# Re-tiling the keys of a causal attention by 128 from the first meta token, in a one-core decoder-block kernel

## The chip, the core and the metric

The kernel runs on one core of one Trainium2 chip. The core has a matrix engine (TensorE, PE in the profile; its weight loads are a row of their own, PEld), a vector engine (VectorE, DVE), a scalar engine (ScalarE, ACT), a general engine (GpSimd, POOL) and a queue engine that issues the transfers (SyncE, SP). The metric is the device time of one execution in microseconds (us). Before the change it is 1646.86 us, the median of 3 runs that lie between 1645.23 and 1648.12 us.

## What is computed

One decoder layer on 1024 tokens of width 1024 with 16 learned meta tokens put ahead of them, so 1040 positions: a norm, one wide projection, three mixers side by side (sliding-window attention with sinks, SWA; forgetting attention, FoX; a gated recurrence), gated sums of their outputs, and a SwiGLU feed-forward. The meta rows are dropped at the end. The change touches FoX, whose core in the reference is

```python
s = jnp.einsum('bqhd,bkhd->bhqk', qi, k).astype(jnp.float32) * (dh ** -0.5)
s = s + ci[..., :, None] - cum[:, :, None, :]
q_pos = n * BLOCK + jnp.arange(BLOCK)
mask = (k_pos[None, :] <= q_pos[:, None]) & (k_pos >= n_pad)[None, :]
s = jnp.where(mask, s, NEG_INF)
p = jax.nn.softmax(s, axis=-1).astype(v.dtype)
return jnp.einsum('bhqk,bkhd->bqhd', p, v)
```

It has 8 heads of 64 channels. Only the 1024 real tokens are queries of the kernel. Query block j holds the real tokens 128j to 128j+127, which are the positions 16+128j to 16+128j+127. With causality it needs the positions 0 to 143+128j: whole tiles of 128 counted from position 0, and 16 keys more, and these last 16 are seen by the last 16 queries of the block alone.

## The kernel before

All products of matrices are made from float32 data that is split in two parts, a rounded high part and the rest (`split`, lines 112 to 125: ACT copies the high part, DVE subtracts it). A projection is three products per tile, high by high, high by low, low by high (`mm3`, line 144, its matmul on line 151).

The part around the change runs from about 223 us to 734 us of the profiled execution. Two Python generators are woven into one program by `drive` (line 233). The main generator gives the projections: queries and keys of each pair of heads, and 24 gate tiles whose results go to memory. The side generator gives the attention, first SWA (mixer 0), then FoX (mixer 1). After each piece of the side (a `yield`), `drive` lets the main generator emit products until their estimated cost, in ns, has filled a gap: 850 in SWA, 480 in FoX (`GAPS`, line 40). A scheduler then sets the final order on each engine; the rows of order below are what it gives.

In FoX a head is worked in four blocks t of 256 queries (two query blocks i of 128 each). `fox_scores` (line 627) multiplies queries by keys, takes the running minimum of the negated scores on DVE, the exponential on ACT and the division by the sum on POOL (line 663); the result `s` has queries on partitions. `fox_values` (line 665) lists the key tiles, and `pv_pieces` (line 552) works them in groups: a group has a PSUM bank `tr`; each 128x128 tile of `s` is transposed into it (line 573); the bank is split into `ph` and `pl` (lines 118, 119 by way of line 576); and two groups later (`LAG`) each key tile is multiplied as `v` tile by `ph` and by `pl` into the bank `ob` (line 562). `v` has the high part of the values in 64 columns and the low part in the other 64, so a weight load of it has 128 columns. Key tile 0 is the 16 meta tokens alone, padded by zero rows of `v` (line 531 writes them on POOL), and key tile c is the positions 16+128(c-1) onwards, so that tile 2t+2 is the diagonal tile of the second query block, and one tile per block is mostly padding. The transposed scores of tile 0 are those of positions 0 to 127, of which rows 16 to 127 meet the zero rows.

A block t before has the tile 0 and the tile 2t+2 in a first group (3 transposes), then the tiles 1 to 2t+1 in groups of two (4 transposes each), the last of them alone (2 transposes): 4t+5 transposes, 2t+2 pairs of products with 256 columns and one pair with 128. Values come back from memory by `load_v` (line 525), two transfers per head on SP.

Of the kernel before, what the change touches and what calls it, by code (L numbers as in the profile page):

```python
# [9 lines left out]
F32 = mybir.dt.float32  # L10
# [6 lines left out]
P = 128  # L17
D = 1024
KT = D // P
NM = 16  # L20
# [16 lines left out]
P_CW, P_CB, P_BR, P_BI, P_LM, P_NF = 0, 16, 20, 24, 28, 32  # L37

LRU_GAP = 3500.0
GAPS = (850.0, 480.0)  # L40
CREDIT = 8
LAG = 2

# [3 lines left out]
def f32(ap):  # L47
    return ap.bitcast(F32)
# [3 lines left out]
def hybrid_block(ctx, tc, h_in, w_in, w_v0, w_v1, w_bd, par, rows, gains, relt, onehot,  # L52
# [51 lines left out]


    gz = dp.tile([24, P, S], F32, name="gz")
    vs = dp.tile([9, P, 10, P], F32, name="vs")
    osp = dp.tile([3, 2, 4, P, S], F32, name="osp")
    h1s = dp.tile([8, P, D], F32, name="h1s")
    cums = dp.tile([8, T], F32, name="cums")  # L110
# [339 lines left out]
    def values(i, src, ncol):  # L450
        vh = rv.tile([P, KT, ncol], F32R, tag="vh", bufs=1, name=nm("vh"))
        vl = rv.tile([P, KT, ncol], F32R, tag="vl", bufs=1, name=nm("vl"))
        for k in range(0, KT, 2):
            raw = wp.tile([P, 2 * ncol], F32, tag="wr", name=nm("wr"))
            dma(raw, src[:, k * ncol:(k + 2) * ncol])
            split(vh[:, k:k + 2], vl[:, k:k + 2], raw.rearrange("p (k c) -> p k c", k=2))
        for t in range(9):
            n = NM if t == 0 else P
            t0 = 0 if t == 0 else NM + (t - 1) * P
            c, off = (0, t0) if t0 < W0 else (1, t0 - W0)  # L460
            ps = mm_bank(f"_v{t}")
            if t == 0:

                for k in range(KT):
                    for a, b in ((meta[:, k], vh), (meta[:, k, :NM], vl)):
                        pe.matmul(ps[:a.shape[-1], :ncol], a, b[:, k], start=k == 0 and b is vh, stop=k == KT - 1,
                                  skip_group_check=True)
                    yield 2 * (ncol / 2.4 + 3)
                low = rv.tile([NM, ncol], F32, tag="low", bufs=1, name=nm("low"))
                act.activation(low, ps[32:32 + NM, :ncol], AF.Copy)  # L470
                dve.tensor_tensor(low, ps[:NM, :ncol], low, ALU.add)
                ps = low
            else:
                yield from mm3(ps[:, :ncol], [(uh[c][:, k, off:off + P], ul[c][:, k, off:off + P],
                                               vh[:, k], vl[:, k]) for k in range(KT)])
            st = rv.tile([P, 5, 2, 64], F32R, tag="vst", bufs=2, name=nm("vst"))
            split(st[:n, :, 0], st[:n, :, 1], ps[:n, :320].rearrange("p (h d) -> p h d", h=5))
            dma(vs[t, :n, 5 * i:5 * i + 5], st[:n].rearrange("p h a d -> p h (a d)"))
            if ncol > 320:
                dve.tensor_tensor(zall[:n, t], ps[:n, 320:328], rowt[:n, 8:16], ALU.add)  # L480

# [8 lines left out]
    with ExitStack() as ctx2:  # L490
# [33 lines left out]
                    dma(x[b], x[a])  # L524

        def load_v(h):

            v = at([P, 9, P], F32R, "v", 2)
            if h == 0:
                pad(r2, 320 + 5632)  # L530
            pool.memset(f32(v[:, 0]), 0.0)
            dma(v[:, 1:], vs[1:, :, h].rearrange("t p c -> p t c"))
            dma(v[:NM, 0], vs[0, :NM, h])
            return v

        def out_sum(ob, ot, h, q0, n):
# [14 lines left out]
        def pv_pieces(pieces, vt, ob):  # L551
# [5 lines left out]

            def pv(todo, ph, pl):
                nonlocal count
                for c, a, b, q0 in todo:  # L560
                    for x in (ph, pl):
                        pe.matmul(ob[:, q0:q0 + b - a], vt[:, c], x[:, a:b],  # L562
                                  start=count == 0, stop=count == n_mm - 1, skip_group_check=True)
                        count += 1

            for grp in pieces:
                tb = tr_bank()
                ph, pl = at([P, 512], F32R, "ph", 3), at([P, 512], F32R, "pl", 3)
                todo, col = [], 0
                for c, cols, q0 in grp:  # L570
                    w0 = col
                    for src in cols:
                        pe.transpose(tb[:, col:col + P], src, ident)  # L573
                        col += P
                    todo.append((c, w0, col, q0))
                split(ph[:, :col], pl[:, :col], tb[:, :col])
                pend.append((todo, ph, pl))
                yield None
                if len(pend) > LAG:
                    pv(*pend.pop(0))  # L580
                    yield None
# [82 lines left out]

        def fox_values(h, t, st, vt, ot):
            ob = o_bank()
            last = 2 * t + 2

            def piece(c):
                k0 = 0 if c == 0 else NM + P * (c - 1)  # L670
                if c == last:
                    return c, [st[1][:, k0:k0 + P]], P
                return c, [st[i][:, k0:k0 + P] for i in range(2)], 0

            pieces = [[piece(0), piece(last)]]
            pieces += [[piece(x) for x in range(c, min(c + 2, last))] for c in range(1, last, 2)]
            yield from pv_pieces(pieces, vt, ob)
            out_sum(ob, ot, h, 256 * t, 256)

# [618 lines left out]
```

## Time and profile before

| | before |
|---|---|
| median of 3 runs (lowest, highest) | 1646.86 us (1645.23, 1648.12) |
| the profiled execution's own time | 1646.19 us |
| its span, first to last instruction | 1644.4 us |
| PE busy | 1623.2 us, 99% |
| PEld busy | 1369.6 us, 83% |
| DVE busy | 997.7 us, 61% |
| ACT busy | 762.1 us, 46% |
| POOL busy | 387.4 us, 24% |
| transposes of `s` (line 573) | 480, from 243.5 to 728.9 us |
| products with `v` (line 562) | 544, from 245.0 to 731.5 us |

A row of a timeline gives the start of an instruction in us from the start of the span, how long it took, the engine, the line of the kernel, the operation, the tile written and those read, rows by columns of the weights, the moving data, and how many equal ones are merged. Matmuls overlap in such rows, since a row lasts until the result is written; what one costs is therefore read from starts: the time from one start to the next. A row of waits names the engine and tile that waited, who released it, the us in total, how many times, and the longest.

### The profile page before, as it was taken

To read this page: it belongs to the slowest core of one execution; us is meant where nothing else is said; L and a number is where in the kernel's file an instruction comes from. 1 tells how busy PE (TensorE), PEld (TensorE's weight loads), DVE (VectorE), ACT (ScalarE), POOL (GpSimd) and SP (SyncE) were. 2 spreads that over 40 slices of the span, in tenths; PEclk is the share of its full clock that TensorE was granted. 3 is DMA by queue.
4 is the path that set the end of the run, shared out by engine and by line. 5 is a ranking of instruction groups with operands and counts; after the bars stand their busy time and mean duration, and the time that the engine had idled before them with its cause. 6 is when DMAs were issued, how large, how long until landed. Compare 5 with 4: busy or idle time off the path is not lost.

```text
span 1644.4 us, 22612 instructions
## 1 busy us (share of the span) xinstructions
PE 1623.2 (99%) x8143; PEld 1369.6 (83%) x8143; DVE 997.7 (61%) x1817; ACT 762.1 (46%) x1402; POOL 387.4 (24%) x322
## 2 busy tenths in 40 slices
PE   7999999999999999999999999999999999999998
PEld 6898988888888888888887888888888888888886
DVE  6556666555566666651339446977777676476554
ACT  6466465545555555542336443433333333355342
POOL 2000001001122221110224100267756666300000
PEclk9999999999999999999999999999999999999999
DMA  7232342223324142329746221345554453697542
GB/s 255 78 104 94 133 139 86 98 72 122 115 72 129 61 123 75 113 97 320 249 144 233 96 91 71 122 149 187 208 193 148 148 175 126 213 367 271 193 128 103
DMA packets 110880, 242.48 MB, mean 147 GB/s; under 512 B 11944, under 2 KB 23544, under 8 KB 110512
## 3 DMA queue, kind: packets, MB, share of 16 engines
q1 hardware_dynamic: 110768, 241.04, 43.2%
q8 instruction: 64, 1.05, 0.3%
q14 instruction: 48, 0.39, 0.1%
HBM read 163.45 MB, written 72.21 MB: 143 GB/s over the span
## 4 chain that ended last, share of the span: by engine, by line
PE 91%; DVE 3%; ACT 2%; DMA 1%; issue 1%; POOL 0%; SPq 0%; DVEq 0%; ACTq 0%; POOLq 0%
PE mm_w L151 27%; PE mm_s L151 13%; PE tr_s L151 7%; PE mm_br L151 6%; PE mm_wo L151 5%; PE mm_x L1162 4%; PE tr_y L1162 4%; PE sc_y L1162 4%; PE mm_v L151 3%; PE ob L562 3%; PE sc_s L151 3%; PE tr L573 3%; PE ob_x L1162 1%; PE mm_g L151 1%; PE mm_u L151 1%
## 5 line engine op out<-in xcount | busy, mean ns | idle before, releaser
L151 PE MATMUL mm_w<-uh,wh 128*128 128x512 f32 (+2 forms) x744 | 292.5, 393 | 0.0
L151 PE MATMUL mm_w<-uh,wl 128*128 128x512 f32 (+2 forms) x744 | 280.4, 377 | 0.0
L151 PE MATMUL mm_w<-ul,wh 128*128 128x512 f32 (+2 forms) x744 | 280.2, 377 | 0.0
L151 PEld LDWEIGHTS mm_w<-uh,wl 128*128 128x128 f32 x744 | 140.0, 188 | 25.7
L151 PEld LDWEIGHTS mm_w<-uh,wh 128*128 128x128 f32 x744 | 140.4, 189 | 12.8
L151 PEld LDWEIGHTS mm_w<-ul,wh 128*128 128x128 f32 x744 | 140.7, 189 | 11.6
L119 DVE TENSOR_TENSOR ab<-raw,ab 128x1024 fp32r<-128x1024 f32 x77 | 92.9, 1223 | 71.1 <-ACT ab L118 70.6
L118 ACT ACTIVATE ab<-raw 128x1024 fp32r<-128x1024 f32 x77 | 80.8, 1059 | 94.5 <-DMA raw<-w_fo_dram 22.1
L118 ACT ACTIVATE wh<-wr 128x1024 fp32r<-128x1024 f32 (+1 forms) x84 | 72.0, 859 | 108.3 <-PE mm_w L151 50.5
L151 PE MATMUL mm_br<-o,wh 128*128 128x512 f32 x384 | 118.3, 389 | 0.0
L151 PE MATMUL mm_s<-pt,ar 128*128 128x512 f32 x492 | 118.2, 389 | 0.0
L119 DVE TENSOR_TENSOR pl<-tr,ph 128x384 fp32r<-128x384 f32 (+2 forms) x160 | 87.4, 555 | 47.1 <-ACT ph L118 43.3
L151 PEld LDWEIGHTS mm_s<-pt,ar 128*128 128x128 f32 x492 | 92.3, 188 | 19.2
L118 ACT ACTIVATE ph<-tr 128x384 fp32r<-128x384 f32 (+2 forms) x160 | 77.0, 486 | 52.8 <-PE tr L573 49.2
L119 DVE TENSOR_TENSOR wl<-wr,wh 128x1024 fp32r<-128x1024 f32 x45 | 55.9, 1242 | 71.9 <-ACT wh L118 71.7
L663 POOL TENSOR_SCALAR s<-s,sm 128x144 f32<-128x144 f32 (+3 forms) x64 | 48.9, 766 | 171.4 <-DVE sm L662 141.4
L151 PEld LDWEIGHTS mm_br<-o,wh 128*128 128x128 f32 x384 | 72.1, 188 | 14.8
L573 PE MATMUL tr<-ident,s 128*128 128x128 f32 x480 | 79.8, 274 | 0.7 <-DVE pl L119 0.2
L151 PE MATMUL mm_wo<-woh,hl 128*128 128x512 f32 x256 | 79.1, 389 | 0.0
L151 PE MATMUL mm_br<-o,wl 128*128 128x512 f32 x192 | 75.2, 392 | 1.5 <-DVE wl L119 1.5
L573 PEld LDWEIGHTS tr<-ident,s 128*128 128x128 f32 x480 | 59.1, 140 | 17.7 <-DVE pl L119 3.4
L1162 PE MATMUL mm_x<-ab 128*128 128x512 f32 x297 | 72.7, 389 | 0.0
(269 smaller groups left out, 3629.3 us busy)
## 6 DMA issues: line engine op xcount, KB each, us to landing
wr<-w_in_dram SPq DMA_DIRECT2D x45, 512.0 KB, 3.6
wr<-w_fi_dram SPq DMA_DIRECT2D x44, 512.0 KB, 4.1
raw<-asp SPq DMA_DIRECT2D x77, 256.0 KB, 3.4
asp<-a SPq DMA_DIRECT2D x66, 256.0 KB, 2.8
gz<-z SPq DMA_DIRECT2D x48, 256.0 KB, 2.1
o<-osp SPq DMA_DIRECT2D x24, 512.0 KB, 5.6
sg<-gz SPq DMA_DIRECT2D x48, 256.0 KB, 3.4
fo<-w_fo_dram SPq DMA_DIRECT2D x22, 512.0 KB, 4.0
```

Source lines behind the costliest of these rows:

```text
L118: a = act.activation(hi, src, AF.Copy)
L119: i = dve.tensor_tensor(lo, src, f32(hi), ALU.subtract)
L151: pe.matmul(ps, a, b, start=first and i == 0, stop=i == n - 1, skip_group_check=not first)
L562: pe.matmul(ob[:, q0:q0 + b - a], vt[:, c], x[:, a:b], start=count == 0, stop=count == n_mm - 1, skip_group_check=True)
L573: pe.transpose(tb[:, col:col + P], src, ident)
L663: pool.tensor_scalar(s[:, :nk], s[:, :nk], den, 1.0, ALU.mult, ALU.mult)
L1162: pe.matmul(banks[x], a[:, 0, q], b[:, 1], start=first and j == 0 and c == 0, stop=j == NJ - 1 and c % 3 == 2, skip_group_check=True)
```

## The change

FoX now counts its key tiles from position 0, so that tile c is the positions 128c to 128c+127 for every c. A block t has the whole tiles 0 to 2t for both query blocks, the tile 2t+1 for the second one, and for each of the two query blocks 16 keys more (`last + i`, 16 rows of `v`), for its last 16 queries. The padded tile 0 is gone from FoX. The 16 by 16 corners are brought across by an ordinary matmul against the last 16 columns of the identity, since only these queries are wanted, and they stand in the same bank behind the whole tiles; two further narrow splits of 16 partitions and 32 columns follow the wide ones. SWA keeps its tiles. The values lie in memory by position, and for the FoX heads POOL writes no zeros. The gap in FoX goes from 480 to 590.

```diff
-GAPS = (850.0, 480.0)
+GAPS = (850.0, 590.0)
...
-    vs = dp.tile([9, P, 10, P], F32, name="vs")
+    vs = dp.tile([T, 10, P], F32, name="vs")
...
-            dma(vs[t, :n, 5 * i:5 * i + 5], st[:n].rearrange("p h a d -> p h (a d)"))
+            dma(vs[t0:t0 + n, 5 * i:5 * i + 5], st[:n].rearrange("p h a d -> p h (a d)"))
...
-            pool.memset(f32(v[:, 0]), 0.0)
-            dma(v[:, 1:], vs[1:, :, h].rearrange("t p c -> p t c"))
-            dma(v[:NM, 0], vs[0, :NM, h])
+            if h < 2:
+
+                pool.memset(f32(v[:, 0]), 0.0)
+                dma(v[:, 1:], vs[NM:, h].rearrange("(t p) c -> p t c", p=P))
+                dma(v[:NM, 0], vs[:NM, h])
+            else:
+
+                dma(v[:, :8], vs[:S, h].rearrange("(t p) c -> p t c", p=P))
+                dma(v[:NM, 8], vs[S:, h])
...
-                for c, a, b, q0 in todo:
+                for c, a, b, q0, nk in todo:
                     for x in (ph, pl):
-                        pe.matmul(ob[:, q0:q0 + b - a], vt[:, c], x[:, a:b],
+                        pe.matmul(ob[:, q0:q0 + b - a], vt[:nk, c], x[:nk, a:b],
...
                     for src in cols:
-                        pe.transpose(tb[:, col:col + P], src, ident)
-                        col += P
-                    todo.append((c, w0, col, q0))
-                split(ph[:, :col], pl[:, :col], tb[:, :col])
+                        nk = src.shape[-1]
+                        if nk == P:
+                            pe.transpose(tb[:, col:col + P], src, ident)
+                            full = col + P
+                        else:
+                            pe.matmul(tb[:nk, col:col + nk], src, ident[:, P - nk:], start=True, stop=True)
+                        col += nk
+                    todo.append((c, w0, col, q0, nk))
+                split(ph[:, :full], pl[:, :full], tb[:, :full])
+                if col > full:
+                    split(ph[:NM, full:col], pl[:NM, full:col], tb[:NM, full:col])
...
-            last = 2 * t + 2
+            last = 2 * t + 1
 
             def piece(c):
-                k0 = 0 if c == 0 else NM + P * (c - 1)
-                if c == last:
-                    return c, [st[1][:, k0:k0 + P]], P
-                return c, [st[i][:, k0:k0 + P] for i in range(2)], 0
-
-            pieces = [[piece(0), piece(last)]]
-            pieces += [[piece(x) for x in range(c, min(c + 2, last))] for c in range(1, last, 2)]
+
+                return c, [st[i][:, P * c:P * c + P] for i in range(c == last, 2)], P * (c == last)
+            pieces = [[piece(c), piece(c + 1)] for c in range(0, last - 1, 2)]
+            pieces += [[piece(last - 1), piece(last)]]
+            pieces[-1] += [(last + i, [st[i][:, P * (last + i):P * (last + i) + NM]], P * (i + 1) - NM) for i in range(2)]
```

The scheduled order shows it on PE in the last block of FoX (head 7, t = 3), before the change. `tr` is the bank of a group, `s` the scores, `ob` the sum of the block, `mm_w` a gate tile, one of whose 24 products a row is.

```order
L562 MATMUL ob_7375<-pl_7443,v_7070 128x256
L573 MATMUL tr_7474<-ident,s_7362 128x128
L573 MATMUL tr_7474<-ident,s_7390 128x128 x2
L151 MATMUL mm_w_1373_7458<-uh_100,wh_7351 128x512
L151 MATMUL mm_w_1373_7458<-ul_102,wh_7351 128x512
L151 MATMUL mm_w_1373_7458<-uh_100,wl_7352 128x512
L573 MATMUL tr_7485<-ident,s_7362 128x128
L573 MATMUL tr_7485<-ident,s_7390 128x128
L573 MATMUL tr_7485<-ident,s_7362 128x128
L573 MATMUL tr_7485<-ident,s_7390 128x128
```

The first group has three transposes, the next ones four. The block closes with a group of two transposes, and, after other groups, with the two products of that last tile:

```order
L573 MATMUL tr_7532<-ident,s_7362 128x128
L573 MATMUL tr_7532<-ident,s_7390 128x128
L151 MATMUL mm_w_1373_7458<-uh_100,wh_7351 128x512
L151 MATMUL mm_w_1373_7458<-ul_102,wh_7351 128x512
L151 MATMUL mm_w_1373_7458<-uh_100,wl_7352 128x512
L562 MATMUL ob_7473<-ph_7498,v_7070 128x256
L562 MATMUL ob_7473<-pl_7499,v_7070 128x256
```

With the change the same block on PE has its group of three last, with the two corners behind it:

```order
L580 MATMUL tr_7475<-ident,s_7308 128x128
L580 MATMUL tr_7475<-ident,s_7350 128x128 x2
L583 MATMUL tr_7475<-ident,s_7308 16x16
L583 MATMUL tr_7475<-ident,s_7350 16x16
L567 MATMUL ob_7431<-ph_7445,v_7033 128x256
L567 MATMUL ob_7431<-pl_7446,v_7033 128x256
```

and the products of that group run in one go, four narrow ones at its end:

```order
L567 MATMUL ob_7431<-ph_7476,v_7033 128x256
L567 MATMUL ob_7431<-pl_7477,v_7033 128x256
L567 MATMUL ob_7431<-ph_7476,v_7033 128x128
L567 MATMUL ob_7431<-pl_7477,v_7033 128x128
L567 MATMUL ob_7431<-ph_7476,v_7033 128x16
L567 MATMUL ob_7431<-pl_7477,v_7033 128x16
L567 MATMUL ob_7431<-ph_7476,v_7033 128x16
L567 MATMUL ob_7431<-pl_7477,v_7033 128x16
L151 MATMUL mm_w_1280_7425<-uh_100,wh_7326 128x512
```

So a block loses two transposes and two products of 256 columns and gains two corners and four products of 16 columns. On POOL, at the change from head 6 to head 7, before:

```order
L663 TENSOR_SCALAR s_6536<-s_6536,sm_6501 128x1040
L717 TENSOR_TENSOR nbd_7076<-nb_7074,cmt 128x1024
L531 MEMSET v_7070 128x128
L663 TENSOR_SCALAR s_6689<-s_6689,sm_6688 128x144
L663 TENSOR_SCALAR s_6698<-s_6698,sm_6688 128x272
```

and with the change, where the zeros are gone from between the bias and the scores:

```order
L675 TENSOR_SCALAR s_6503<-s_6503,sm_6452 128x1040
L727 TENSOR_TENSOR nbd_7038<-nb_7036,cmt 128x1024
L675 TENSOR_SCALAR s_6659<-s_6659,sm_6658 128x144
L675 TENSOR_SCALAR s_6668<-s_6668,sm_6658 128x272
L675 TENSOR_SCALAR s_6761<-s_6761,sm_6760 128x400
```

More of the change, by code (lines that the diff above doesn't have):

```diff
@@ L568, in pv_pieces @@
                 ph, pl = at([P, 512], F32R, "ph", 3), at([P, 512], F32R, "pl", 3)
-                todo, col = [], 0
+                todo, col, full = [], 0, 0
                 for c, cols, q0 in grp:
```

## The prediction

> **What bounds the kernel now.** I read the page's busy times and its chain first, then the stretch of FoX by itself.
>
> ```profile
> PE 1623.2 (99%) x8143; PEld 1369.6 (83%) x8143; DVE 997.7 (61%) x1817; ACT 762.1 (46%) x1402; POOL 387.4 (24%) x322
> PE 91%; DVE 3%; ACT 2%; DMA 1%; issue 1%; POOL 0%; SPq 0%; DVEq 0%; ACTq 0%; POOLq 0%
> 430.70:731.60 300.90, 299.89 (x1796) 260.66 (x1795) 191.61 (x616) 164.91 (x347) 64.69 (x77) 1.00 0.31 95
> ```
>
> The last row is the stretch from the first FoX scores to the last FoX product, with PE, PEld, DVE, ACT and POOL in this order: PE is busy for 299.9 of 300.9 us, DVE for 64%, ACT for 55%. The waits of PE and of its weight loads that concern this part are
>
> ```profile
> PE ob L562 <- ACT q L506: 0.5, 1, 0.5
> PE sc L647 <- DVE sm L654: 0.4, 2, 0.2
> PE ob L562 <- ACT ph L118: 0.3, 1, 0.3
> PEld tr L573 <- DVE pl L119: 3.4, 9, 0.7
> PEld tr L573 <- POOL s L663: 0.7, 3, 0.2
> ```
>
> About 5 us in all, and most of that is weight loads that waited while a product ran. A busy PE alone proves little, since its ends are modelled; the starts do, below: they follow each other without holes. So the stage is a queue of PE instructions, and what the change is worth is the sum of their prices, 32 times (8 heads, 4 blocks t).
>
> **Prices from starts.**
>
> ```profile
> 707.67 0.39 PE L151 MATMUL mm_w<-ul,wh 128*128 128x512 f32 x1
> 707.90 0.39 PE L151 MATMUL mm_w<-uh,wl 128*128 128x512 f32 x1
> 708.13 0.38 PE L573 MATMUL tr<-ident,s 128*128 128x128 f32 x2
> 708.27 0.48 PE L151 MATMUL mm_w<-uh,wh 128*128 128x512 f32 x1
> 708.58 0.40 PE L151 MATMUL mm_w<-ul,wh 128*128 128x512 f32 x1
> 708.82 0.40 PE L151 MATMUL mm_w<-uh,wl 128*128 128x512 f32 x1
> 709.05 0.28 PE L562 MATMUL ob<-ph,v 128*128 128x256 f32 x1
> 709.18 0.28 PE L562 MATMUL ob<-pl,v 128*128 128x256 f32 x1
> 709.29 0.22 PE L562 MATMUL ob<-ph,v 128*128 128x128 f32 x1
> 709.35 0.27 PE L562 MATMUL ob<-pl,v 128*128 128x128 f32 x1
> 709.46 0.33 PE L562 MATMUL ob<-ph,v 128*128 128x256 f32 x1
> 709.63 0.28 PE L562 MATMUL ob<-pl,v 128*128 128x256 f32 x1
> 709.75 0.29 PE L562 MATMUL ob<-ph,v 128*128 128x256 f32 x1
> 709.88 0.28 PE L562 MATMUL ob<-pl,v 128*128 128x256 f32 x1
> ```
>
> A product of 512 columns takes 0.232 from start to start (707.67 to 708.13, 708.58 to 709.05). From 707.90 to 708.58 lie two of them and two transposes: 0.68 - 0.464 = 0.216, so a transpose costs 0.108, though the product behind it shows its start only 0.14 after. A product of 256 columns costs 0.1175 (709.63 to 709.75 to 709.88). From 709.29 to 709.63 lie two of 128 columns and one of 256: 0.34 - 0.118 = 0.222, so 0.111 for 128 columns, hardly less than for 256. Scores with 144 columns tell why:
>
> ```profile
> 286.57 0.39 PE L151 MATMUL mm_w<-uh,wl 128*128 128x512 f32 x1
> 286.80 0.23 PE L599 MATMUL sc<-k,q 128*128 128x144 f32 x1
> 286.86 0.27 PE L600 MATMUL sc<-k,q 128*128 128x144 f32 x1
> 286.97 0.45 PE L151 MATMUL mm_w<-uh,wh 128*128 128x512 f32 x1
> 287.26 0.40 PE L151 MATMUL mm_w<-ul,wh 128*128 128x512 f32 x1
> ```
>
> 0.69 - 0.464 = 0.226, so 0.113 for 144 columns and 0.111 for 128: below 256 columns the price doesn't follow the columns. What is the same in these products is a weight load of 128 columns, and only one load can be hidden behind one product. I take 0.108 as the floor of a product whose weights have 128 columns.
>
> **What a block loses:** two transposes, 2 x 0.108 = 0.216, and two products of 256 columns, 2 x 0.1175 = 0.235; together 0.451 us, 14.4 us over 32 blocks. No change of this size can save more than that.
>
> **What a block gains, the narrow products.** Four products with 16 rows of `v`, 128 columns of weights and 16 columns moved. No row before has that form with rounded operands. The nearest are the transposes of the meta rows in the first microseconds, when PE ran at half pace:
>
> ```profile
> 9.08 0.45 PE L205 MATMUL tr<-ident,xg 128*128 128x128 f32 x1 [9.08 <-DVE xg L302]
> 9.08 1.30 PE L205 MATMUL tr<-ident,xg 128*128 128x128 f32 x5 [9.08 <-DVE xg L302]
> 12.31 0.28 PE L205 MATMUL tr<-ident,xg 16*128 16x16 f32 x1
> 12.31 0.60 PE L205 MATMUL tr<-ident,xg 16*128 16x16 f32 x4
> 17.37 0.43 PE L151 MATMUL mm_w<-uh,x0h 128*128 128x272 f32 x1
> 17.59 0.43 PE L151 MATMUL mm_w<-ul,x0h 128*128 128x272 f32 x1
> 20.13 0.29 PE L151 MATMUL mm_w<-ul,x0h 128*128 128x272 f32 x1
> 20.25 0.29 PE L151 MATMUL mm_w<-uh,x0l 128*128 128x272 f32 x1
> ```
>
> (The pairs of rows at 9.08 and at 12.31 are one timeline cut at two places.) A product of 272 columns takes 0.22 at 17 us and 0.12 at 20 us: that is the half pace. In it a full transpose takes (1.30 - 0.45)/4 = 0.213, and one of 16 rows and 16 columns (0.60 - 0.28)/3 = 0.107. So 16 rows are not free even there. If that price halves at full pace like the others, a narrow product costs 0.053; if it is the load, with rounded operands, 0.108. The shortest distance between starts in the quoted rows is 0.06 (286.80 to 286.86, 709.29 to 709.35), but that is paid back by the next; the bottom I allow is half of 0.053, 0.027. I take 0.108, because 128 and 144 columns moved already stood on a floor that fewer columns don't lower, and the load has as many columns as theirs. Four: 0.432; bounds 0.108 and 4 x 0.111 = 0.444.
>
> The Trainium skill, "TensorE: Matmul & The Clock Gate", section "LDWEIGHTS (loading the stationary operand)", has a rule that speaks against this change: a load takes the columns over 1.2 in ns, and the rows don't count, so 16 rows of 128 columns would take 107 ns like a full tile. By it the four cost 0.427, the sum below moves by 0.2 us in all; the floor of 0.111 to 0.113 above agrees, the 16 rows themselves no row shows at full pace. The section "Back-to-back issue gap" of the same page gives about 60 cycles (25 ns) for up to 64 columns moved; by that alone the four would cost 0.1, which is the first rival's far end.
>
> **The two corners.** They are ordinary float32 products. The one that the kernel has is on line 322:
>
> ```profile
> L322 PE MATMUL sc<-oh,rt x2: 803/820/838, 10.9 to 11.5; 32*8 32x383 f32 x2
> ```
>
> The program has it once, the trace twice: it runs as two records 0.6 us apart, 383 columns at half pace, about 1.6 ns a column each. With 16 columns that is nearly nothing, so a record costs its least step. That is 0.027 to 0.053 (the halves above), with weights of 16 columns only, loaded behind it. Two corners are four records; three are paid at that step, and behind the last one the next full load of 0.108 stands open, since there is no long product to hide it: 0.081 + 0.108 = 0.189 to 0.159 + 0.108 = 0.267. I take the middle, 0.228. Bounds: 4 x 0.027 = 0.108, and 4 x 0.108 = 0.432 if each record pays a full load.
>
> **The sum on PE.** Per block -0.451 + 0.432 + 0.228 = +0.209; over 32 blocks +6.7 us. The bounds are -0.451 + 0.108 + 0.108 = -0.235, -7.5 us, and -0.451 + 0.444 + 0.432 = +0.425, +13.6 us.
>
> **What lies beside it, at nothing.** The wide splits and the zeros on POOL:
>
> ```profile
> L119 DVE TENSOR_TENSOR pl<-tr,ph 128x384 fp32r<-128x384 f32 (+2 forms) x160 | 87.4, 555 | 47.1 <-ACT ph L118 43.3 <-DMA osp<-pl 2.4
> L118 ACT ACTIVATE ph<-tr 128x384 fp32r<-128x384 f32 (+2 forms) x160 | 77.0, 486 | 52.8 <-PE tr L573 49.2 <-PE mm_w L151 1.6 <-ACT z L751 0.7
> POOL v L531 <- PE ob L562: 72.8, 8, 19.3
> ```
>
> 160 wide splits become 128, and 32 narrow ones come. ACT and DVE are covered by the gate products (DVE 64%, ACT 55% busy); uncovered, a narrow split would add its ACT and DVE step ahead of the narrow products (second rival). POOL waited 72.8 us to write zeros, with the division of the next scores queued behind. That queue comes free, but PE waited for the divisions only 0.7 us, so at most that is won. The loads of `v` on SP are the same in number and bytes, and stand in the same places. The wider gap cancels out: a FoX head has 14 yields of scores and 28 of values before, 20 of values now, so 336 x 480 = 161,280 of gap becomes 272 x 590 = 160,480, and in the scheduled order 195 gate products are left behind the last product with `v`, where 189 were. So the side's end stays covered; if it didn't, each uncovered piece would show as a wait of PE for `pl`.
>
> **Forecast.** The profiled execution took 1646.2 (1644.4 of it the span); +6.7 gives 1652.9. It is 0.7 below the median of the runs, well inside their 2.9, so against the median: **1653.5 us**.
>
> **Rivals.** First, **the 16 rows are cheap**: the load of 16 rows is shorter than that of 128. For it: the half-pace transposes at 0.107 against 0.213. Against it: those also move 16 columns instead of 128, which explains the half as well. At 0.053 a block gets -0.451 + 0.212 + 0.228 = -0.011, 1646.5 us. It ends faster from the point where four narrow products and two corners cost less than 0.451; with the corners at 0.108 too, it is -0.131, 1642.7 us, and at the bottom 1639.4 us. Chance 0.17, of which 0.11 lies below 1643.6.
>
> Second, **PE waits for the narrow split**: a block with t = 0 has one group now, and its narrow products need a second ACT and a second DVE step. For it: the order puts other work of ACT between the wide and the narrow split in places. Against it: three quarters of the blocks have two or more groups in flight, and the first four products of the group, 0.235 + 0.222 = 0.46 us, run meanwhile. If in every block about 0.2 us stays uncovered, that is 6.4 us more: 1660 us. Chance 0.09.
>
> Third, **the corners are dear**: each of four records pays a full load, 0.432 instead of 0.228, +13.1 us in all: 1660 us. For it: two records, each with a load of its own. Against it: loads of 8 to 16 columns. Chance 0.10.
>
> **How the numbers follow.** The forecast has 0.64, with a range of its own from 1649 to 1657 (corners between 0.108 and 0.267, narrow products between 0.09 and 0.111). Below 1643.6 (0.2% of 1646.9 is 3.3, about what a measurement of this kernel can tell from no change) lies 0.11, all from the first rival; within 0.2% the rest of it and the forecast's low edge, 0.06 + 0.15 = 0.21; above 1650.2 the remaining 0.68. The range that leaves out no more than 2 in 10 goes from 1645, into the first rival, to 1660, where the other two stand.
>
> **What would show it.** Right: in the changed trace, four narrow products in a row with starts about 0.108 apart and the 512-column product behind them late by as much; each corner as two records; no new wait of PE for `ph`, `pl` or `s`; DVE and ACT busy time lower; every stage behind FoX shifted alike. Wrong: narrow products 0.03 to 0.06 apart (first rival), rows of PE or PEld waiting for `pl` by some us (second), corners with 0.2 each (third), or a stage elsewhere that changed its length.

## The result, and the profile after

The changed kernel takes 1667.18 us, the median of 5 runs (1664.48 to 1670.19); the kernel before, run beside it, 1646.86. The ratio is 1.0129, with a 95% interval from 1.0118 to 1.0140. It is slower, by 20.3 us where 6.7 were forecast, and outside the range of 1645 to 1660.

The page of the changed kernel gives the busy time of each engine, and rows of its waits from 429 to 748 us tell what held the weight loads in FoX (us in total, times, longest):

```profile
PE 1642.0 (99%) x8271; PEld 1379.4 (83%) x8271; DVE 991.4 (60%) x1817; ACT 759.3 (46%) x1402; POOL 385.4 (23%) x314
```

```profile
PEld tr L583 <- issue: 4.9, 29, 0.2
PEld ob L567 <- ACT ph L118: 2.1, 6, 0.4
PEld tr L580 <- DVE pl L119: 1.6, 4, 0.4
PEld tr L580 <- POOL s L675: 1.1, 5, 0.3
PEld ob L567 <- DVE pl L119: 1.0, 4, 0.3
```

PE's share of 99% is what it was. DVE, ACT and POOL have less to do. Waits for `ph`, `pl` and `s` stay near the size they had, 5.8 us here and 5.4 before, and PE itself has no row of waits in this window. One large row is new, and "issue" means that it names nobody: before the corners (`tr L583`) the weight loads stood idle 29 times, 4.9 us in all, about 0.17 each, with no instruction to wait for.

A table by stretch places the loss. Its columns are the stretch, and then for PE, PEld, DVE, ACT and POOL the busy time and the number of instructions, then the clock and the transfers. Of the kernel before, the attention (from the first scores of SWA to the first `mm_br`) and all that is behind it:

```profile
223.50:774.50 551.00, 548.95 (x3099) 470.11 (x3099) 317.56 (x924) 283.96 (x634) 87.49 (x114) 1.00 0.35 114
774.50:1637.20 862.70, 861.18 (x3820) 710.39 (x3819) 544.50 (x657) 346.53 (x572) 289.11 (x193) 1.00 0.51 174
```

and of the changed one FoX alone, the attention, and what is behind it:

```profile
429.20:747.90 318.70, 318.29 (x1918) 270.52 (x1916) 186.15 (x616) 161.02 (x345) 62.92 (x70) 1.00 0.29 91
222.00:792.40 570.40, 568.93 (x3228) 481.29 (x3228) 312.33 (x924) 281.48 (x634) 85.45 (x106) 1.00 0.34 111
792.40:1655.50 863.10, 861.33 (x3820) 710.37 (x3819) 543.46 (x657) 346.63 (x571) 289.09 (x193) 1.00 0.51 174
```

FoX went from 300.9 to 318.7 us, the attention with it from 551.0 to 570.4, that is +19.4 us, and the stages behind it take 863.1 where they took 862.7. Of the 19.4, 1.6 lie between FoX and the first `mm_br`, where 195 gate products are left instead of 189: the six had stood in FoX before. So the loss is made in FoX and handed on unchanged. (The two spans differ by 18.3 only, since the part ahead of the attention took 1.5 us less in this execution.) The clock is 1.00 throughout.

The timeline of the changed kernel on PE, at the close of one block and at the corners of the next group, shows how:

```profile
737.34 0.40 PE L151 MATMUL mm_w<-uh,wl 128*128 128x512 f32 x1
...
737.87 0.27 PE L567 MATMUL ob<-pl,v 128*128 128x128 f32 x1
738.07 0.27 PE L567 MATMUL ob<-ph,v 16*128 16x16 f32 x1
738.20 0.25 PE L567 MATMUL ob<-pl,v 16*128 16x16 f32 x1
...
738.43 0.25 PE L567 MATMUL ob<-pl,v 16*128 16x16 f32 x1
738.61 0.50 PE L151 MATMUL mm_w<-uh,wh 128*128 128x512 f32 x1
738.94 0.39 PE L151 MATMUL mm_w<-ul,wh 128*128 128x512 f32 x1
...
743.98 0.49 PE L580 MATMUL tr<-ident,s 128*128 128x128 f32 x3
744.40 0.27 PE L583 MATMUL tr<-ident,s 128*16 128x16 f32 x4
744.59 0.39 PE L567 MATMUL ob<-ph,v 128*128 128x256 f32 x1
744.82 0.28 PE L567 MATMUL ob<-pl,v 128*128 128x256 f32 x1
```

Between themselves the narrow products step by 0.11 to 0.13, as forecast. But from the last product with 128 rows to the first with 16 it is 0.20 (737.87 to 738.07), and from the last narrow one to the 512-column product 0.18 (738.43 to 738.61), where 0.11 was expected at both. To price all four, take the whole group between two 512-column products. From 737.34 to 738.94 it is 1.60; less two 512-column products, 0.464, the group costs 1.14 us. The same order of two 256-column and two 128-column products without narrow ones costs 0.455, the median of 24 such groups in the experiment without narrow work, below. One of them, from that trace:

```profile
714.84 0.40 PE L151 MATMUL mm_w<-uh,wl 128*128 128x512 f32 x1
...
715.76 0.39 PE L151 MATMUL mm_w<-ul,wh 128*128 128x512 f32 x1
```

It takes 0.92, and 0.456 without the 512-column products. So the four narrow products cost **0.685 us, not 0.432**.

At the corners three transposes should take 0.324, but 0.42 pass from 743.98 to 744.40: a hole of 0.10. The four records themselves take 0.19 to the next start, of which 0.106 follow the last record. Then the product behind takes a further 0.22 to 0.23 instead of 0.1175, so the way out costs about 0.1 more than the one open load. Of 743.98 to 744.82, 0.84, the three transposes and one 256-column product explain 0.44; the pair of corners costs 0.40 here, and **0.390 us, not 0.228** in the median of the 16 such groups that stand between two 512-column products (0.7215 against 0.332 for three bare transposes).

A block is then -0.451 + 0.685 + 0.390 = +0.624, and 32 of them +20.0 us. The attention shows 19.4, the medians 20.3. The arithmetic closes to within 1 us; what remains is why these two prices are what they are.

### The profile page after: what moved, and what is told of

It is laid out like the page before. It is cut to its first block, busy times and chain, and to the rows that moved or that the text cites. A ratio compares the mean times of both kernels' runs of the same rounds, so it can differ in the third digit from the quotient of the medians.

```text
span 1662.7 us, 22854 instructions
## 1 busy us (share of the span) xinstructions
PE 1642.0 (99%) x8271; PEld 1379.4 (83%) x8271; DVE 991.4 (60%) x1817; ACT 759.3 (46%) x1402; POOL 385.4 (23%) x314
## 4 chain that ended last, share of the span: by engine, by line
PE 92%; DVE 3%; ACT 2%; DMA 1%; issue 1%; POOL 0%; SPq 0%; DVEq 0%; POOLq 0%; ACTq 0%
PE mm_w L151 28%; PE mm_s L151 13%; PE tr_s L151 7%; PE mm_br L151 6%; PE mm_wo L151 5%; PE ob L567 4%; PE mm_x L1172 4%; PE tr_y L1172 4%; PE sc_y L1172 4%; PE mm_v L151 3%; PE sc_s L151 3%; PE tr L580 3%; PE ob_x L1172 1%; PE mm_g L151 1%; PE mm_u L151 1%; PE sc L659 1%
## 5 line engine op out<-in xcount | busy, mean ns | idle before, releaser
L119 DVE TENSOR_TENSOR pl<-tr,ph 128x384 fp32r<-128x384 f32 (+2 forms) x160 | 80.4, 506 | 54.1 <-ACT ph L118 52.8
L118 ACT ACTIVATE ph<-tr 128x384 fp32r<-128x384 f32 (+2 forms) x160 | 71.0, 447 | 54.2 <-PE tr L580 19.4
L567 PE MATMUL ob<-ph,v 128*128 128x256 f32 (+2 forms) x304 | 76.2, 270 | 1.2 <-ACT q L506 0.5
L567 PE MATMUL ob<-pl,v 128*128 128x256 f32 (+2 forms) x304 | 76.5, 276 | 0.1
```

What stands on the lines that cost most here:

```text
L118: a = act.activation(hi, src, AF.Copy)
L119: i = dve.tensor_tensor(lo, src, f32(hi), ALU.subtract)
L567: pe.matmul(ob[:, q0:q0 + b - a], vt[:nk, c], x[:nk, a:b], start=count == 0, stop=count == n_mm - 1, skip_group_check=True)
```

## Experiments: is it the narrow work, and what in it?

The theory after the result: PE stops for some 0.1 us when it goes from weights with 128 rows to weights with 16, and again on the way back, and something like it happens at the corners. Its rivals: a narrow product is dear by itself (by its 16 columns moved, or by its weight load); the gap, the layout or the loads lose the time; or the corners are dear because they are ordinary float32 products.

**Without narrow work.** The corners, the narrow splits and the narrow products are left out, so each query block misses its last 16 keys; layout, gap and loads are those of the change.

```diff
-            pieces[-1] += [(last + i, [st[i][:, P * (last + i):P * (last + i) + NM]], P * (i + 1) - NM) for i in range(2)]
```

> No corners, no narrow splits, no narrow products: the 16 last keys of a block are left out, so the output is not the reference's; tiles, gaps and layout as in the changed kernel. If all the loss is in the narrow work, the block only loses two transposes and two products of 256 columns, 0.451 us, and the time is 1646.9 - 14.4 = 1632.5 us. If the wider gap, the layout of the values or fewer groups in flight cost something, it is as much above that.

1632.43 us, ratio 0.9913 (0.9898 to 0.9927), 14.3 us under the kernel before. That is the forecast's 32 x 0.451 = 14.4 to a tenth, and 34.8 us under the changed kernel. All of the loss lies in the narrow work; the layout of the values, the wide splits and the loads cost nothing that shows. The gap was also put back by itself:

```diff
-GAPS = (850.0, 590.0)
+GAPS = (850.0, 480.0)
```

> The changed kernel with the gap of FoX at 480 again, nothing else. Theory: the gap only says where the gate products stand among the attention's, and PE is never short of either, so 1667 within 2 us. Rival: with the smaller gap the side ends earlier or later and PE waits for it more: over 1670; or the wider gap was itself part of the loss: under 1664.

1666.03 us, ratio 1.0119 (1.0104 to 1.0134): the gap makes no difference that can be told, either way.

**Rows of the narrow products.** The four narrow products take 128 rows of `v` and of `ph`, and still move 16 columns. They then multiply the wrong keys, and read the wide split and not the narrow one; number, columns moved and weight columns are kept.

```diff
+                        vk, xk = vt[:nk, c], x[:nk, a:b]
+                        if nk < P:
+                            vk, xk = vt[:, c - 1], x[:, :nk]
-                        pe.matmul(ob[:, q0:q0 + b - a], vt[:nk, c], x[:nk, a:b],
+                        pe.matmul(ob[:, q0:q0 + b - a], vk, xk,
```

> The four narrow products of a block keep their 16 columns but use 128 rows: they multiply a whole value tile by 16 columns of the wide part, so the output is not the reference's; everything else is as in the changed kernel. Theory A, the number of rows: PE stops when it goes from weights of 128 rows to weights of 16 rows and back. Then the four cost about 4 x 0.11 = 0.44 instead of the 0.68 us seen after the change, 32 x 0.24 = 7.6 us less than the changed kernel's 1667.2, so 1659.6, and the 0.2 us step ahead of the first narrow product falls to 0.11. Theory B, the 16 columns: products too short to hide the next load cost more than the load. Then nothing changes: 1667, and the step of 0.2 stays.

1660.53 us, ratio 1.0078 (1.0061 to 1.0094), 6.7 us under the changed kernel. Its timeline:

```profile
739.49 0.39 PE L151 MATMUL mm_w<-uh,wl 128*128 128x512 f32 x1
...
740.01 0.28 PE L570 MATMUL ob<-pl,v 128*128 128x128 f32 x1
740.12 0.22 PE L570 MATMUL ob<-ph,v 128*128 128x16 f32 x1
740.20 0.26 PE L570 MATMUL ob<-pl,v 128*128 128x16 f32 x1
...
740.42 0.26 PE L570 MATMUL ob<-pl,v 128*128 128x16 f32 x1
740.53 0.48 PE L151 MATMUL mm_w<-uh,wh 128*128 128x512 f32 x1
740.85 0.39 PE L151 MATMUL mm_w<-ul,wh 128*128 128x512 f32 x1
```

The step in is 0.11 (740.01 to 740.12), the step out 0.11 (740.42 to 740.53). The group is 1.36 - 0.464 = 0.90, the four products 0.446 (median of 24 groups): the forecast's 4 x 0.111. So with 16 rows the same products cost 0.24 us more, 7.6 us over 32 blocks. The step in and the step out account for 0.09 and 0.07 of it; the rest stands in the step behind each (0.13 for 0.08, and 0.33 for 0.32).

The counterpart keeps 16 rows and moves 128 columns instead of 16, into the first 128 columns of the bank, so these sums are wrong too.

```diff
+                        xk, ok = x[:nk, a:b], ob[:, q0:q0 + b - a]
+                        if nk < P:
+                            xk, ok = x[:nk, :P], ob[:, :P]
-                        pe.matmul(ob[:, q0:q0 + b - a], vt[:nk, c], x[:nk, a:b],
+                        pe.matmul(ok, vt[:nk, c], xk,
```

> The mirror: the four narrow products keep 16 rows, but move 128 columns into the bank instead of 16 (the output is not the reference's). Theory A (rows): the steps into and out of the 16 rows stay, the four cost 0.68 or a little more, 1667 to 1669 us. Theory B (columns): they cost what products of 128 columns cost, 0.44, 1659.6 us.

1669.04 us, ratio 1.0134 (1.0119 to 1.0149). Its timeline on PE:

```profile
738.70 0.27 PE L570 MATMUL ob<-pl,v 128*128 128x128 f32 x1
738.90 0.32 PE L570 MATMUL ob<-ph,v 16*128 16x128 f32 x1
...
739.29 0.27 PE L570 MATMUL ob<-pl,v 16*128 16x128 f32 x1
739.49 0.49 PE L151 MATMUL mm_w<-uh,wh 128*128 128x512 f32 x1
```

0.20 on the way in (738.70 to 738.90) and 0.20 on the way out (739.29 to 739.49) are still there. The four cost 0.738, only 0.05 more than with 16 columns. The rows decide, the columns moved hardly matter.

Is it the small number of rows, or any number other than 128? The first of these two edits again, with 64 rows:

```diff
+                            vk, xk = vt[:64, c - 1], x[:64, :nk]
```

> As the run with 128 rows in the narrow products, but with 64 rows (values of the wrong keys, so the sums differ; count and columns are those of the changed kernel). If any change of the row count stops PE, the four products cost 0.68 us like those of 16 rows, and the time is about 1667 us. If it is only small counts (the 16 rows), they cost 0.44 us like those of 128 rows, and the time is about 1660.5 us.

1664.94 us, a single run; the trace decides here:

```profile
738.43 0.27 PE L570 MATMUL ob<-pl,v 128*128 128x128 f32 x1
738.64 0.27 PE L570 MATMUL ob<-ph,v 64*128 64x16 f32 x1
...
738.99 0.25 PE L570 MATMUL ob<-pl,v 64*128 64x16 f32 x1
739.17 0.49 PE L151 MATMUL mm_w<-uh,wh 128*128 128x512 f32 x1
```

0.21 in and 0.18 out, 0.688 for the four: as with 16 rows. Half a tile already stops PE. These products read the wide split, as those with 128 rows did, so a wait for the narrow split is not what the 16 rows cost.

The trace of the kernel before has one row of this kind at full clock, which the prediction did not use: a transpose of 16 rows on line 443. First PE, then the weight loads:

```profile
148.72 0.39 PE L151 MATMUL mm_w<-uh,wl 128*128 128x512 f32 x1
149.04 0.38 PE L443 MATMUL tr<-ident,lf 16*8 16x16 f32 x2
```

```profile
149.03 0.19 PEld L443 LDWEIGHTS tr<-ident,lf 16*8 16x8 f32 x2 [0.35 <-issue]
```

(The x2 merges it with the transpose behind it.) The step in is 0.32 where a 512-column product takes 0.232, 0.09 too much, and the queue of loads stood idle for 0.35 us ahead of it with nobody named. It is a single row, and shows the way in alone. The eight transposes of the same line with 128 rows and as many weight columns have no such row.

The Trainium skill has this rule on a page that the prediction did not use, "TensorEngine Tiling (Array Packing)", section "Key Properties": "Changing tiling mode (not just tile) drains the TensorE". The traces fit it: a group with 16 or 64 rows costs 0.24 us more than the same with 128. The page gives no price, and speaks of modes that one chooses; here the kernel chose none, and that the row count alone selects one is a reading of the traces, not something they print.

**The corners.** They are brought across by transposes instead: 16 columns of weights as before, but 128 columns moved, and into the end of the bank. The narrow split then reads another place there, so the values used are not those of the corner.

```diff
-                            pe.matmul(tb[:nk, col:col + nk], src, ident[:, P - nk:], start=True, stop=True)
+                            pe.transpose(tb[:nk, 512 - P:], src, ident)
...
-                    split(ph[:NM, full:col], pl[:NM, full:col], tb[:NM, full:col])
+                    split(ph[:NM, full:col], pl[:NM, full:col], tb[:NM, 480:])
```

> The two 16 by 16 corners are done as transposes of the 16 score columns for all 128 queries (both into the same place, so the first block's corner is lost and the output is not the reference's), not as ordinary float32 products; the narrow products stay. Theory: a corner costs 0.195 us because PE leaves the transposes for another kind of weights and runs it in two records; as a transpose it costs 0.108, so a block loses 0.39 - 0.216 = 0.17, 5.6 us, 1661.6 us, and the hole of 0.17 ahead of the first corner goes. Rival: the hole is a wait for the scores or for the bank; then it stays and the time stays at 1667.

1660.54 us, ratio 1.0084 (1.0067 to 1.0101), 6.6 us under the changed kernel. On PE:

```profile
739.66 0.49 PE L580 MATMUL tr<-ident,s 128*128 128x128 f32 x3
739.99 0.38 PE L583 MATMUL tr<-ident,s 128*16 128x128 f32 x2
740.12 0.36 PE L567 MATMUL ob<-ph,v 128*128 128x256 f32 x1
```

Three transposes take 0.33 to the next start: no hole. The pair costs 0.224 (median of 16 groups), two transposes at 0.112, against 0.390. With both edits together:

> Both cures at once: corners as transposes of 16 columns by 128 queries (into one place), narrow products on 128 rows of other data; the output is not the reference's. If the prices of e1 and e3 add, a block loses 0.451 and gains 0.44 + 0.22, +0.21, 32 x 0.21 = 6.7 us over the kernel before: 1653.5 us. If the two cures share one cost (one stop of PE serves both), less is gained: between 1655 and 1660.

1652.51 us, ratio 1.0033 (1.0019 to 1.0047). The two prices add, and this kernel is the forecast's own sum: products at 0.111 and a pair at 0.224, for which it gave 1653.5.

What in the ordinary product makes the hole: its 16 weight columns, or its kind? A last one keeps the kind and gives it 128 columns of weights, the tile ahead of the corner (the whole tile is multiplied, and rows 0 to 15 of the result are those of other keys).

```diff
+                            wide = src
+                        if nk == P:
...
-                            pe.matmul(tb[:nk, col:col + nk], src, ident[:, P - nk:], start=True, stop=True)
+                            pe.matmul(tb[:, col:col + nk], wide, ident[:, P - nk:], start=True, stop=True)
```

> The corners stay ordinary float32 products of 16 columns moved, but have 128 columns of weights (the scores of the whole tile before), so only the width of the weights differs from the changed kernel; the output is not the reference's. Theory, a narrow array: the hole of 0.17 ahead of the first corner and the late product behind the last come from weights of 16 columns, as with the 16 rows; then both go, and each of the four records costs about a load, 0.11, 0.43 a pair against 0.39: 1666 to 1670 us. Rival, the kind of product: going from transposes to an ordinary float32 product makes the hole, so it stays and the pair costs 0.17 more: over 1672.

1666.88 us, a single run. Its timeline:

```profile
746.38 0.49 PE L582 MATMUL tr<-ident,s 128*128 128x128 f32 x3
746.71 0.52 PE L585 MATMUL tr<-ident,s 128*128 128x16 f32 x4
747.07 0.36 PE L567 MATMUL ob<-ph,v 128*128 128x256 f32 x1
```

The hole is gone (0.33 from 746.38 to 746.71, and no row of a weight load waiting for nothing), but the four records now take 0.36 where those of the narrow weights took 0.19. The pair costs 0.445 in the median of 15 groups. So an ordinary float32 corner pays in one of two ways: four records with full loads, or four cheap ones with a stop ahead of them and behind them. Only in this kind of product do 16 columns of weights stop PE: the transposes above have 16 as well and show no hole, and the trace of the kernel before shows none for rounded products with 48 and 16 weight columns, at full clock:

```profile
94.37 0.31 PE L466 MATMUL mm_v<-vh,meta 128*48 128x328 f32 x1
94.52 0.31 PE L466 MATMUL mm_v<-vl,meta 128*16 128x328 f32 x1
94.67 0.31 PE L151 MATMUL mm_v<-vh,uh 128*128 128x328 f32 x1
94.82 0.31 PE L151 MATMUL mm_v<-vl,uh 128*128 128x328 f32 x1
```

From 48 to 16, from 16 to 128 and from 128 to 128 weight columns the step is 0.15 each time. Why only the ordinary float32 product stops is open.

## Experiments: a version without narrow shapes

If only full-size shapes are used, the layout without the padded tile should win. All ends of a head (8 query blocks, 16 keys each) are gathered: the divided scores of the last 16 keys of each block go to a tile `cs` of 128 queries by 8 x 16 columns. One transpose turns it, DVE keeps the last 16 queries and spreads them by a mask so that each end meets its own keys, and two products of 128 columns with one `v` tile of the 128 end keys give the sums, which DVE adds to the block's last 16 queries. The result is that of the reference.

```diff
+            pe.transpose(tb[:, :P], cs, ident)
+            q = tb[:, P - NM:P].rearrange("p (j q) -> p j q", j=1).to_broadcast([P, NB, NM])
+            dve.tensor_tensor(xm[:, 0].rearrange("p (j q) -> p j q", j=NB), q,
+                              bm.rearrange("p (j q) -> p j q", j=NB), ALU.mult)
+            split(ph[:, :P], pl[:, :P], xm[:, 0])
...
+            for i, x in enumerate((ph, pl)):
+                pe.matmul(ob[:, :P], vt[:, 8], x[:, :P], start=i == 0, stop=i == 1)
...
+                pool.tensor_scalar(cs[:, NM * j:NM * j + NM], s[:, nk - NM:nk], den, 1.0, ALU.mult, ALU.mult)
```

> A whole version, meant to give the reference's output. The last 16 keys of all 8 query blocks of a head are gathered: POOL writes those 16 score columns of each block into one 128 by 128 tile, which is transposed once per head; DVE spreads its last 16 queries over a block diagonal with a mask; two products of 128 rows and 128 columns with the 8 x 16 value rows give the rest of the head's output, which DVE adds. Gap 545. By the measured prices a head loses 4 x 0.451 and gains 0.108 + 0.222, 8 x 1.47 = 11.8 us: 1635 us. Rival: the chain from transpose over DVE, ACT and DVE to the two products, or the two POOL steps per block instead of one, makes PE wait at the end of each head: above 1638; with 0.5 us a head 1639.

A miss: 1673.73 us, ratio 1.0166 (1.0151 to 1.0181). FoX itself took 297.3 us, 3.5 less than before. The time was lost behind it, as the waits of PE and of ACT show:

```profile
PE mm_br L152 <- ACT wh L119: 26.3, 1, 26.3
```

```profile
ACT wh L119 <- DMA wb<-w_br_dram: 25.0, 1, 25.0
```

ACT waited 25 us for the first weights of the next stage, and PE with it; the loads of `o` ahead of them in SP's queue waited too. The mask had a tile of 512 bytes ahead of the attention's buffers, which moved those behind it; that this held the loads up is a reading that no run tests by itself. In the second try the new tiles lie where the kernel has a filler, DVE and not POOL scales the end columns, a pause between the split and the products is left out, and the gap is 560:

```diff
-GAPS = (850.0, 545.0)
+GAPS = (850.0, 560.0)
...
-    bm = cp.tile([P, P], F32, name="bm")
...
+                ends_mask.append(at([P, P], F32, "bm", 1))
...
-            yield None
...
+                dve.tensor_scalar(cs[:, NM * j:NM * j + NM], s[:, nk - NM:nk], den, None, ALU.mult)
...
-                pool.tensor_scalar(cs[:, NM * j:NM * j + NM], s[:, nk - NM:nk], den, 1.0, ALU.mult, ALU.mult)
```

> The version with the ends of a head gathered, mended in two places that the trace of v1 shows: its new tiles stand at the place of the old filler on the right side, so that nothing on the left moves (v1 lost 26.3 us ahead of the branch products, where a load of the outputs waited for a tile that had moved), and DVE instead of POOL scales the 16 end columns (POOL's step of 0.28 us stood between the scores and the transposes, which waited 5.5 us for it in 15 places). Gap 560. Price theory: 1635 us, with up to 4 us of waits 1639. Rival: the branch stage still waits for its loads: over 1655.

1644.41 us, ratio 0.9990 (0.9981 to 1.0000): 22.8 us under the changed kernel, and no difference from the kernel before that can be told. The late weights are gone; which of the four edits did it was not separated. With the gap at 600:

```diff
-GAPS = (850.0, 560.0)
+GAPS = (850.0, 600.0)
```

> The same with a gap of 600: more gate products between the pieces, so splits are ready earlier, and some 60 gate products fewer left behind the attention. Theory: the waits of products for their splits shrink, 1 to 3 us less than v2. Rival: with 126 instead of 183 gate products left, 29 us, the loads of the branch stage come late and it is slower than v2.

1657.56 us, ratio 1.0066 (1.0049 to 1.0082). More gate products are spent inside FoX, and those left behind it, 125 in the trace where 183 were left at 560, no longer cover the next weights:

```profile
PEld mm_br L151 <- ACT wh L118: 11.1, 1, 11.1
```

So the gap matters after all once it eats the cover; from 480 to 590 in the change it did not.

At 560 the products of the ends waited for their split. Last, the transpose, mask and split are therefore given out ahead of the last block's values:

```diff
-                                prev = both(prev, fox_ends(h, cs, vt, ot))
+                                xs = []
+                                prev = both(fox_ends(h, cs, vt, ot, xs), prev, fox_add(h, vt, ot, xs))
```

> As the version with the ends gathered per head and gap 560 (1644.4 us), but the transpose, the mask and the split of the gathered ends are given out ahead of the last block's values, and only their two products stand behind these; the split parts have tiles of their own in the left-over space. Result unchanged. There the two products of the ends waited 5.3 us in all (0.8 + 3.0 us for ph, 0.5 us for pl, 0.6 us issue, and small ones). If these waits are real time of PE, 3 to 5 us go: 1640 us, 0.3 to 0.4% under the kernel before. Rival: the transpose now waits for the column that DVE scales last (cs), since it stands right behind the scores; then the wait only moves from the products to the transpose, and the time stays at 1644 us.

1644.46 us, ratio 0.9989 (0.9980 to 0.9998), at most 0.2% under the kernel before, and nothing won on the version with the ends last. The longer waits of the weight loads at the ends and around them, first with the ends last, then with them early:

```profile
PEld tr L588 <- POOL s L708: 3.3, 9, 0.5
PEld ob L665 <- ACT ph L118: 3.0, 7, 0.7
```

```profile
PEld tr L589 <- POOL s L712: 5.5, 12, 0.6
PEld tr L589 <- DVE xm L660: 1.8, 4, 1.2
PEld ob L669 <- DVE o L555: 1.2, 4, 0.5
```

The wait for `ph` went, and waits for `s`, for the mask's `xm` and for the bank came: the rival's kind of end, a wait that only moves. These versions stay 12 us above the one without narrow work, of which the ends' own instructions, 8 x (0.108 + 2 x 0.111), explain 2.6. Small waits of this kind are seen, but the rest was not settled piece by piece.

## Why the prediction was wrong

- **The bound** (a queue of PE instructions, the sum of their prices) was right. PE has no row of waits in FoX after the change, and the sum of the measured prices gives 20.0 us of 20.3.
- **What a block loses**, 0.451 us, was right: 14.3 us by experiment, 14.4 by the sum.
- **The narrow products, taken at 4 x 0.108 = 0.432, is the step that failed first.** They cost 0.685. The floor of a load of 128 columns was right, as 0.446 with 128 rows shows, and so was the reasoning that fewer columns moved don't help. But it was read from products that all have 128 rows, and its upper bound, 4 x 0.111, assumed that a change of rows costs nothing between products. The prediction says that no row shows 16 rows at full pace, and turns to rows at half pace in the first microseconds. That is not so: the transpose on line 443 at 149.04 us, shown above, is such a row, and it came 0.09 late, after 0.35 in which the weight loads stood idle. The half-pace rows gave only the step from one 16-row transpose to the next, not the way in or out. The bound should have been left open upwards. The missing term, 0.253 a block, is 8.1 us.
- **The corners, taken at 0.228, are the second.** Their four records were cheap, about as thought, and the load behind them was late, as thought. What was left out is the stop: 0.10 ahead of them, and about as much again on the way out, where the products behind are late by nearly two loads (0.106 and 0.105 us) and not by one. 0.390 against 0.228 is 5.2 us. The ordinary float32 product of line 322, from which the prediction took its two records, had such a wait in the trace of before (0.3 us on "issue" at half pace), but there the rows change as well. The third rival named the right place and nearly the price (0.432, four full loads), but its mechanism is that of the wide corner, not of this one.
- 8.1 + 5.2 = 13.3, and 6.7 + 13.3 = 20.0: no other step is needed. The corners' error alone would have left the time inside the range (1658.7), the narrow products' alone just beyond it (1661.6); both went the same way.
- **At nothing**: splits, zeros on POOL, loads and gap were rightly put at nothing (-14.3 us without narrow work; 1666.03 with the old gap). The first rival (16 rows cheap) has the wrong sign. The second (PE waits for the narrow split) is not seen: in all of FoX the weight loads of the products with `v` waited 3.1 us for `ph` and `pl`, against 2.6 without any narrow split, and PE itself not at all.
- The rule of the Trainium skill that the prediction cites ("TensorE: Matmul & The Clock Gate", section "LDWEIGHTS (loading the stationary operand)"), that a load goes by its columns and not its rows, agrees with the traces: a load of 16 rows took 0.18 to 0.19 us and one of 128 rows 0.19, and the narrow products step by 0.11 to 0.13. It says nothing of the way into and out of them, and there the cost lay.

## What to carry to other kernels

Price a small product not only by its columns and its load, but by the change of shape to its neighbours: here 0.24 us for each visit to weights of 16 or 64 rows, which four narrow products after one another pay once. Keeping the small shape at 128 rows (0.446 against 0.685 us for the four), or gathering it over many blocks into full products (1644.4 against 1667.2 us), was cheaper here than cutting it out; but the gathering brings its own splits and waits, and it ended level with the padded tile. Search the whole trace for the shape that is added, also in stages far from the change, and read how it is entered and left. Where no row has it, the upper bound must hold the cost of going there, not only of being there.

## What of the hardware was not expected

- Weights of 64 rows stop PE as much as those of 16 (0.688 and 0.685 us for four products), against 0.446 with 128 rows.
- With 16 rows, moving 128 columns instead of 16 costs 0.05 us on four products.
- Float32 transposes with 16 columns of weights cost 0.112 each and show no stop. Ordinary float32 products with 16 show one of 0.10 ahead of them, and with 128 columns none. Rounded products with 48 and 16 weight columns show none either (steps of 0.15 us for 328 columns moved, as with 128 weight columns).
